# A quarter of the normalized tokens is made again from the raw tokens instead of being stored and loaded

## The chip, the core and the metric

The kernel runs on one core of one Trainium2 chip. The metric is the device time in microseconds of one execution. The core has five engines with queues of their own: TensorE (PE in the profile, with its weight loads as PEld), VectorE (DVE), ScalarE (ACT), GpSimd (POOL) and SyncE (SP), which here only issues transfers. Transfers of all queues run on 16 DMA engines.

## The reference

One step of one layer: 4096 new tokens and 64 sample tokens (8 sequences of 8), 1024 wide, all in float32.

```python
def _rmsnorm(x, g):
    xf = x.astype(jnp.float32)
    r = lax.rsqrt(jnp.mean(xf * xf, axis=-1, keepdims=True) + RMS_EPS)
    return (xf * r).astype(x.dtype) * g
...
    h = _rmsnorm(x, g_pre)
    z = h @ w_in
    cb, cc, ch, cg, q, k, v, ag, mq, mg = _split_cols(z)
    u = cc * ch
    up = jnp.concatenate([conv_buf, u], axis=1)
    conv = conv_w[0] * up[:, 0:t] + conv_w[1] * up[:, 1:t + 1] + conv_w[2] * up[:, 2:t + 2]
    out_a = jax.nn.silu(cg) * cb * conv
...
    out_b = jax.nn.silu(ag) * o_b
    o_c = _mem_attend(mq.reshape(n, t, MEM_HEADS, HEAD_DIM), mem_k, mem_v)
    out_c = jax.nn.silu(mg) * o_c
    y = jnp.concatenate([out_a, out_b, out_c], axis=-1) @ w_out
    return x + _rmsnorm(y, g_post), new_conv, new_k, new_v
```

`o_b` is windowed attention (128 keys back, with a sink for each head), `_mem_attend` is attention to 256 memory tokens. The change concerns the first two lines of the layer: the normalized tokens `h` and their product with `w_in` (1024 by 2816 columns).

## The kernel before, in words

The product `h @ w_in` is computed in three phases, each for some of the columns of `w_in`: phase 0 and phase 1 take four pairs of 128 columns each, phase 2 three (`PHASES`). In a phase, all 4160 tokens pass in 8 blocks of 520. A block's tokens, transposed so that the 1024 channels lie on the partitions, are cut into four quarters `B11`, `B12`, `B21`, `B22`: the first number says which half of the channels, the second which half of the 520 tokens. A quarter is a tile of 128 partitions by 4 by 260 elements (520 KB).

The block's product is made by Strassen's scheme in Winograd's form, with 7 products in place of 8 (`PRODUCTS`, numbered p = 0 to 6): the right operands are `B11`, `B21`, `T2`, `T3`, `T1`, `B22`, `T4`, where `T1 = B12 - B11`, `T2 = B22 - T1`, `T3 = B22 - B12` and `T4 = B21 - T2` (`t_sum`, one VectorE subtraction each). `B12` is thus no operand of a product itself: only `T1` and `T3` read it. In the first two blocks of phase 0 (`PLAIN_BLOCKS`) the eight plain products are made instead. Each operand is split into a high and a low part (`split`: a ScalarE cast to `hi`, a VectorE subtraction to `lo`), so each step p is 4 column pairs times 12 matmuls (line 368), 48 matmuls in phases 0 and 1. Two sets of `hi` and `lo` exist: the split for step p + 1 is made while step p is multiplied. The accumulated banks are taken out and added by `evict` (VectorE line 375, ScalarE line 377).

In phase 0 a quarter is loaded raw from the input (`x_load`, line 238; the input lies in chunks of 384 tokens, so a quarter comes in one or two pieces), multiplied by the gains of the norm (`gain`, line 326, four ScalarE instructions), then by the row factors `rb` (`scale`, line 335, one VectorE instruction), and stored normalized to `hd` in DRAM (POOL's queue, line 164). The row factors are made in phase 0 from sums of squares, stored to `rowd`, and spread over the partitions by a transfer (`rows_load`, line 251). For block 2 they are made in another way, by a matmul (`rows_product`), and not stored. In phase 1 the blocks 2 to 7 load their four normalized quarters from `hd` (line 530); blocks 0 and 1 make theirs as in phase 0. The differences `T1` to `T4` of phase 1 are stored to `hd` too, for phase 2.

`B12` and `B22` lie in a tile `place` with room for one block. `T3` is written over `B12` in it, so the next block's `B12` is loaded after the split of `T3`, as a job of step 4 (`next_block`). Its use is `T1`, at the end of step 6.

What sets the order: in phase 0 every engine runs in the order in which the code is written. From phase 1 on (`store_queue[0] = DMA`), stores go by SP's queue, and a scheduler with costs of its own arranges the instructions; those in `in_turn` and `keep_in_program_order` keep the place in which they were written. Each engine and queue then works strictly in that order. Small tiles of phase 1 (weight sums, convolution tiles, the row factors of block 1) come from a pool of 9 buffers (`temp`).

## Time and profile before

| | |
|---|---|
| median of 3 runs | 1526.55 us (1522.49 to 1528.41) |
| the profiled execution's own time | 1528.73 us |
| its span, first to last instruction | 1527.0 us |
| phase 0, Strassen blocks 2 to 7 | about 103 to 346 us |
| phase 1 | about 346 to 668 us, blocks 2 to 7 from about 426 us |
| phase 2 | about 668 to 936 us |
| attention and output | about 936 us to the end |
| busy: PE, PEld, DVE, ACT, POOL | 99%, 91%, 79%, 55%, 26% of the span |
| DMA | 319.71 MB, mean 209 GB/s |

The phases' times are those at which the first matmul of their operands stands in the timeline. A busy PE is not PE at its peak, since matmuls overlap; what a reader should look at is whether a matmul waits, and for whom. In the trace the names of operands are shortened: `lo_5T` is the low part of one of the differences of block 5, `x_6B` a quarter of block 6, `hd_B` a stored quarter. Names of phase 0 and phase 1 look alike, and the time tells them apart.

### The profile page before, as it was taken

What the parts mean: (1) busy time and instruction counts of PE and PEld (TensorE: products, weight loads), DVE (VectorE), ACT (ScalarE), POOL (GpSimd) and SP (SyncE); (2) the same over time, 40 slices, a digit from 0 to 9 for tenths busy, and PEclk for the clock granted to TensorE, in tenths of its full rate; (3) what the DMA queues carried; (4) which work ended last, traced back from release to release, by engine and by line L of the source; (5) the groups of instructions that cost most, each with busy time, mean ns of one, the idle gap of its engine ahead of it and who ended that gap; (6) DMA issues with size and microseconds to landing.
All of it is one profiled execution on the core that took longest, in us unless ns stands there. A gap on an engine that the chain in (4) does not pass through costs nothing.

```text
span 1527.0 us, 30947 instructions
## 1 busy us (share of the span) xinstructions
PE 1507.6 (99%) x11497; PEld 1384.4 (91%) x11497; DVE 1199.3 (79%) x2089; ACT 843.5 (55%) x2066; POOL 398.5 (26%) x576
## 2 busy tenths in 40 slices
PE   9999999999999999999999999999999999999997
PEld 8999999999999999999999999777888788888875
DVE  5779887899988777897677768777877788878874
ACT  5776665566322222354455536666666666666652
POOL 0223322211400000000111311234445544455641
PEclk9999999999999999999999999999999999999999
DMA  9989999978855333478687698988765555666552
GB/s 258 168 250 221 289 290 259 265 243 303 209 183 182 118 121 126 161 235 295 222 261 232 213 305 254 282 241 235 201 169 160 156 164 161 175 171 170 153 196 75
DMA packets 217322, 319.71 MB, mean 209 GB/s; under 512 B 37397, under 2 KB 143381, under 8 KB 217141
## 3 DMA queue, kind: packets, MB, share of 16 engines
q1 hardware_dynamic: 196837, 273.54, 60.8%
q0 software_dynamic: 19616, 43.15, 10.5%
q8 instruction: 91, 1.49, 0.4%
q10 hardware_dynamic: 720, 1.05, 0.2%
q14 instruction: 58, 0.48, 0.1%
HBM read 208.50 MB, written 110.15 MB: 209 GB/s over the span
## 4 chain that ended last, share of the span: by engine, by line
PE 75%; DMA 11%; DVE 6%; issue 4%; POOL 2%; ACT 1%; SPq 1%; DVEq 0%; ACTq 0%; POOLq 0%
PE c L368 39%; PE y_c L1746 16%; PE y L1637 3%; PE ws L1331 3%; DMA nat<-in_x_p 2%; DMA md<-th 2%; PE wo L1394 2%; PE wo L1059 2%; PE xs L1353 2%; PE xt L1366 2%; PE wt L1376 2%; PE wo L1388 2%; DMA place<-in_xt 1%; DMA wr_3A<-in_w_in 1%; DMA hd_B<-place 1%
## 5 line engine op out<-in xcount | busy, mean ns | idle before, releaser
L375 DVE TENSOR_TENSOR z<-c,z 128x520 f32<-128x520 f32 (+1 forms) x308 | 194.6, 645 | 83.5 <-PE c L368 82.5
L1746 PE MATMUL y_c<-wo,pw 128*128 128x512 f32 (+1 forms) x636 | 158.9, 392 | 0.6 <-DVE yn L1784 0.6
L1287 ACT ACTIVATE sm<-sm,wnm 128x128 f32<-128x128 f32 x256 | 99.4, 389 | 72.0 <-DVE wnm L1281 72.0
L1746 PEld LDWEIGHTS y_c<-wo,pw 128*128 128x128 f32 x636 | 114.0, 188 | 27.8 <-issue 5.4
L1190 POOL TENSOR_SCALAR xp<-xp,xrd 128x256 f32<-128x256 f32 x128 | 71.8, 577 | 196.9 <-DVE xrd L1184 192.3
L1178 ACT ACTIVATE xp<-xs,xnm 128x256 f32<-128x256 f32 x128 | 59.0, 473 | 38.3 <-DVE xnm L1170 22.9
L737 POOL CAST wmask<-negs 128x256 uint8<-128x256 f32 x1 | 1.1, 1149 | 266.6 <-DMA negs<-in_wmask 266.6
L1637 PE MATMUL y<-wo,mh 128*128 128x512 f32 x192 | 64.5, 398 | 0.2 <-ACT y L1646 0.2
L1310 POOL TENSOR_SCALAR_AFFINE_SELECT wpv<-wpt 128x512 f32<-128x512 f32 x62 | 56.9, 939 | 8.7 <-ACT wpt L1305 8.4
L1313 POOL TENSOR_SCALAR_AFFINE_SELECT wpt<-wpt 128x512 f32<-128x512 f32 x64 | 46.3, 742 | 38.6 <-ACT wpt L1305 38.2
L1331 PE MATMUL ws<-kst,q 128*128 128x256 f32 (+1 forms) x480 | 55.7, 297 | 0.0
L1341 DVE COPY_PREDICATED sm<-wmask,ws 128x512 f32<-128x512 uint8 x60 | 40.5, 729 | 19.0 <-ACT sm L1340 19.0
L276 ACT ACTIVATE nat<-nat 104x1024 f32<-104x1024 f32 x40 | 42.3, 1058 | 23.6 <-DMA nat<-in_x_p 23.5
L1658 DVE SCALAR_TENSOR_TENSOR xr<-yn,yst,xr 128x1024 f32<-128x1024 f32 (+2 forms) x35 | 51.3, 1470 | 2.9 <-POOL yst L1653 2.8
L407 ACT CAST zh<-z 128x520 fp32r<-128x520 f32 x56 | 33.3, 624 | 34.6 <-DVE z L375 31.9
L377 ACT COPY z<-c 128x520 f32<-128x520 f32 (+1 forms) x44 | 24.4, 554 | 50.5 <-PE c L368 47.2
L1331 PEld LDWEIGHTS ws<-kst,q 128*128 128x128 f32 (+1 forms) x480 | 46.4, 187 | 4.1
L1287 ACT ACTIVATION_READ_ACCUMULATOR sm<-sm,wnm 128x1 f32 x256 | 47.9, 187 | 0.0
L1295 DVE TENSOR_TENSOR sm<-sm,wrd 128x512 f32<-128x512 f32 x64 | 44.5, 696 | 1.1
L1746 PE MATMUL y_c<-wo,pc 128*128 128x512 f32 (+1 forms) x162 | 45.2, 400 | 0.0
L164 POOL DMA_DIRECT2D md<-th x48 | 26.3, 549 | 71.3 <-DVE th L425 61.0
L1637 PEld LDWEIGHTS y<-wo,mh 128*128 128x128 f32 x192 | 36.1, 188 | 8.9 <-issue 1.0
(1037 smaller groups left out, 5556.9 us busy)
## 6 DMA issues: line engine op xcount, KB each, us to landing
q<-qd SPq DMA_DIRECT2D x168, 128.0 KB
xr<-in_x_p SPq DMA_DIRECT2D x32, 512.0 KB
nat<-in_x_p SPq DMA_DIRECT2D x39, 416.0 KB
o_yp<-xr SPq DMA_DIRECT2D x31, 512.0 KB
kst<-qd SPq DMA_DIRECT2D x112, 128.0 KB
md<-th POOLq DMA_DIRECT2D x48, 260.0 KB, 7.2
qd<-zh SPq DMA_DIRECT2D x48, 260.0 KB
qd<-z SPq DMA_DIRECT2D x48, 260.0 KB
```

The costliest lines, as they stand in the source:

```text
L368: TE.matmul(bank[:, :HW], l, r, start=first and i == 0, stop=last and i == 3 * KH - 1)
L375: add = lambda dst, other: V.tensor_tensor(dst, c, other, op=ALU.add)
L1178: S.activation(p[:, i, :], s[:, i, :], AF.Exp, bias=nm[:, i : i + 1], scale=SCALE, accum_out=den[:, i : i + 1])
L1190: G.tensor_scalar(p[:, i, :], p[:, i, :], self.rds[h][:, i : i + 1], 0.5, op0=ALU.mult, op1=ALU.mult)
L1287: S.activation(sm[:, hh, :], sm[:, hh, :], AF.Exp, bias=nm[:, hh : hh + 1], scale=SCALE, accum_out=den[:, hh : hh + 1])
L1295: V.tensor_tensor(sm, sm, rd.unsqueeze(2).to_broadcast([P, 4, P]), op=ALU.mult)
L1310: G.affine_select(pv.rearrange("p (h q) -> p h q", h=4), p3, pattern=[[0, 4], [-1, P]], compare_op=ALU.is_gt, fill=0.0, base=0, channel_mu ...
L1313: G.affine_select(p3, p3, pattern=[[0, 4], [1, P]], compare_op=ALU.is_ge, fill=0.0, base=0, channel_multiplier=-1)
L1331: TE.matmul(out(kvh, col, bank), q(kvh, col, bank)[r], k(kvh, part)[r], start=first, stop=True, skip_group_check=not first, **place)
L1637: TE.matmul(acc, self.hl[l][:, k], wo[k][p][:, r], start=k + i == 0, stop=k + i == KT + 1)
L1658: x = V.scalar_tensor_tensor(self.xr[:m, cs], yn[:m, cs], st[:m, 3:4], self.xr[:m, cs], op0=ALU.mult, op1=ALU.add)
L1746: TE.matmul(acc, a[:, l, k], w[:, r, cs], start=first, stop=k == len(ws) - 1 and i == 2, skip_group_check=not new)
```

## The change

`hd` has no `B12` any more. In phase 0 the blocks 2 to 7 don't store it (six transfers of 520 KB fewer on POOL's queue), and block 2 now stores its row factors as well. In phase 1 the blocks 2 to 7 load `B12` raw, spread the row factors (one transfer of 260 KB for each block, at step 1), and multiply by gains and factors at step 6, like blocks 0 and 1.

```diff
@@ -71,7 +71,7 @@
-    hd = [{o: tc.dram_tile([P, KH, HW], F32, name=f"hd{b}_{o}") for o in ("B12", *(o for _, o in PRODUCTS))}
+    hd = [{o: tc.dram_tile([P, KH, HW], F32, name=f"hd{b}_{o}") for _, o in PRODUCTS}
           for b in range(NBLK)]
@@ -283,10 +283,8 @@
             if b in (0, PLAIN_BLOCKS):
                 nat["factors"] = r
-            if b == PLAIN_BLOCKS:
-                return
             G.dma_start(rowd[b].rearrange("(i p) -> p i", p=RG), r[:RG, 0:5])
-            if b > 0:
+            if b > 0 and b != PLAIN_BLOCKS:
                 row_spreads[b] = 4
@@ -333,7 +331,7 @@
     def scale(x, b, o):
         rb = rows[b][:, HW * (int(o[2]) - 1) : HW * int(o[2])]
         in_turn(V.tensor_tensor(x, x, rb.unsqueeze(1).to_broadcast([P, KH, HW]), op=ALU.mult))
-        if b >= PLAIN_BLOCKS or o != "B12":
+        if o != "B12":
             store(hd[b][o], x)
@@ -522,8 +520,12 @@
+    def is_raw(ph, b, o):
+
+        return ph == 0 or b < PLAIN_BLOCKS or o == "B12"
+
     def x_of(ph, b, o, parts=KH):
-        if ph == 0 or b < PLAIN_BLOCKS:
+        if is_raw(ph, b, o):
             t = x_load(ph, b, o, parts)
         else:
             t = x_tile(ph, b, o)
@@ -531,11 +533,11 @@
     def x_gain(ph, b, o):
-        if ph == 0 or b < PLAIN_BLOCKS:
+        if is_raw(ph, b, o):
             gain(xs[ph, b][o], o)
     def x_scale(ph, b, o):
-        if ph == 0 or b < PLAIN_BLOCKS:
+        if is_raw(ph, b, o):
             scale(xs[ph, b][o], b, o)
@@ -556,7 +558,7 @@
-        if p == 1 and nph == 1 and nb < PLAIN_BLOCKS:
+        if p == 1 and nph == 1:
             jobs.append(lambda: rows_load(nb, nb > 0))
```

Up to the new function `is_raw` the changed kernel's lines have numbers 2 lower, behind it 2 higher: gain, scale, split and evict are lines 324, 333, 356 and 357, and 373. In the rows below, a name like `x1_5B21` is phase 1, block 5, quarter B21, and the last number only tells tiles apart; `z1_4_0_1` is an output tile of block 4, `c1_4_0_6` the bank of its step 6, `ub`, `tail`, `cacc` belong to the convolution, `ws10` to the weight sums for phase 2.

SP's queue in phase 1, block 1 (steps 2 to 4), where the weight sums are loaded. Before:

```order
L166 DMA md_149<-cacc0_0_5169 128x456
L201 DMA ws10A21_5335<-in_w_in 128x512
L201 DMA ws10A22_5337<-in_w_in 128x512
L201 DMA ws10A11_5339<-in_w_in 128x512
L201 DMA ws10A12_5341<-in_w_in 128x512
L530 DMA place_159<-hd2_B12_99 128x1040
L166 DMA hd1_T4_98<-x1_1B21_4884 128x1040
L166 DMA md_149<-cacc0_1_5264 128x456
L530 DMA x1_2B21_5374<-hd2_B21_101 128x1040
```

and now:

```order
L166 DMA md_141<-cacc0_0_5156 128x456
L251 DMA rb2_5262<-rowd2_77 128x520
L201 DMA ws10A21_5324<-in_w_in 128x512
L201 DMA ws10A22_5326<-in_w_in 128x512
L201 DMA ws10A11_5328<-in_w_in 128x512
L201 DMA ws10A12_5330<-in_w_in 128x512
L238 DMA place_151<-in_xt 128x4x172
L166 DMA hd1_T4_96<-x1_1B21_4871 128x1040
L166 DMA md_141<-cacc0_1_5224 128x456
L532 DMA x1_2B21_5363<-hd2_B21_98 128x1040
L238 DMA place_151<-in_xt 128x4x88
```

The spread of the row factors stands ahead of the loads of the weight sums, and the second piece of `B12` stands behind the load of `B21`. In the blocks after it the spread stands at the same step, and the one or two pieces of `B12` stand where the one load stood.

ScalarE in phase 1, at the end of block 4 (step 6), for block 5. Before:

```order
L438 ACTIVATE cth4_0_6922<-z1_4_0_0_6618 128x520
L358 CAST hi1_5B11_6905<-x1_5B11_6608 128x4x260
L438 ACTIVATE cth4_1_6938<-z1_4_2_0_6645 128x520
L471 ACTIVATE cacc4_0_7009<-ub4_0_7004,convw_71 128x520
L358 CAST hi1_5B21_6970<-x1_5B21_6787 128x4x260
```

and now:

```order
L436 ACTIVATE cth4_0_6935<-z1_4_0_0_6628 128x520
L356 CAST hi1_5B11_6918<-x1_5B11_6618 128x4x260
L436 ACTIVATE cth4_1_6951<-z1_4_2_0_6655 128x520
L324 ACTIVATE place_151<-place_151,gpre_61 128x260 x4
L356 CAST hi1_5B21_6988<-x1_5B21_6799 128x4x260
L469 ACTIVATE cacc4_0_7027<-ub4_0_7022,convw_71 128x520
```

The four gains stand ahead of the cast of `B21`, and the convolution's first product has moved behind that cast.

VectorE at the same place. Before:

```order
L375 TENSOR_TENSOR z1_4_0_1_6530<-c1_4_0_6_6909,z1_4_0_1_6530 128x2x260
L446 SCALAR_TENSOR_TENSOR z1_4_0_0_6618<-z1_4_0_1_6530,z1_4_0_0_6618 128x520
L456 TENSOR_TENSOR ub4_0_7004<-z1_4_0_0_6618,z1_4_0_1_6530 128x520
L458 COPY tail4_0_7007<-ub4_0_7004 128x2
L455 COPY ub4_1_7029<-tail3_1_6588 128x2
L473 SCALAR_TENSOR_TENSOR cacc4_0_7009<-ub4_0_7004,convw_71,cacc4_0_7009 128x520
L375 TENSOR_TENSOR z1_4_2_1_6570<-c1_4_2_6_6941,z1_4_2_1_6570 128x2x260
L348 TENSOR_TENSOR x1_5T1_6967<-place_159,x1_5B11_6608 128x1040
L359 TENSOR_TENSOR lo1_5B21_6971<-x1_5B21_6787,hi1_5B21_6970 128x4x260
L348 TENSOR_TENSOR x1_5T2_6988<-place_159,x1_5T1_6967 128x1040
```

and now:

```order
L373 TENSOR_TENSOR z1_4_0_1_6540<-c1_4_0_6_6922,z1_4_0_1_6540 128x2x260
L333 TENSOR_TENSOR place_151<-place_151,rb5_6682 128x1040
L444 SCALAR_TENSOR_TENSOR z1_4_0_0_6628<-z1_4_0_1_6540,z1_4_0_0_6628 128x520
L454 TENSOR_TENSOR ub4_0_7022<-z1_4_0_0_6628,z1_4_0_1_6540 128x520
L373 TENSOR_TENSOR z1_4_2_1_6580<-c1_4_2_6_6954,z1_4_2_1_6580 128x2x260
L346 TENSOR_TENSOR x1_5T1_6985<-place_151,x1_5B11_6618 128x1040
L357 TENSOR_TENSOR lo1_5B21_6989<-x1_5B21_6799,hi1_5B21_6988 128x4x260
L346 TENSOR_TENSOR x1_5T2_7006<-place_151,x1_5T1_6985 128x1040
L456 COPY tail4_0_7025<-ub4_0_7022 128x2
L471 SCALAR_TENSOR_TENSOR cacc4_0_7027<-ub4_0_7022,convw_71,cacc4_0_7027 128x520
```

The scaling of `B12` has come in ahead of the convolution's gate, and two copies and the convolution's second product have moved from ahead of `T1` to behind `T2`. The matmuls stand in the same order as before.

## The prediction

> **What bounds the kernel.** I read the busy times by stretch first. In the fence the columns are the stretch, its length, the busy us of PE, PEld, DVE, ACT and POOL with the number of instructions, PE's clock, the share of the DMA engines and GB/s. The first row is phase 0 and the start of phase 1, the next three are block 1 of phase 1, and the last holds most of the blocks whose `B12` changes.
>
> ```profile
> 110.00:395.00 285.00, 282.79 (x2373) 281.75 (x2373) 249.03 (x308) 174.76 (x303) 77.61 (x121) 1.00 0.92 256
> 395.00:400.00 5.00, 5.00 (x44) 5.00 (x44) 5.00 (x9) 1.07 (x1) 4.66 (x7) 1.00 1.12 89
> 400.00:420.00 20.00, 19.71 (x166) 19.50 (x165) 16.79 (x26) 4.51 (x5) 4.67 (x5) 1.00 0.93 326
> 420.00:425.00 5.00, 5.00 (x44) 5.00 (x43) 4.20 (x7) 1.60 (x2) 0.00 (x0) 1.00 0.02 7
> 440.00:640.00 200.00, 200.00 (x1669) 200.00 (x1668) 155.13 (x212) 55.13 (x65) 0.00 (x0) 1.00 0.41 140
> ```
>
> PE is busy in 200.00 of 200 us of phase 1 and in 282.79 of 285 us of phase 0. In phase 0 the DMA engines are 92% busy; in phase 1 they are 41% busy, VectorE 78% (155.13 of 200), ScalarE 28%. So TensorE bounds both phases, and what the change can win or lose is what TensorE waits for. I read its waits next: first from 100 to 400 us (in all: us, times, longest), then from 395 to 700 us, where there is one.
>
> ```profile
> PE c L368 <- DVE lo_6B L359: 0.9, 1, 0.9
> PE c L368 <- ACT hi_6B L358: 0.9, 1, 0.9
> PE c L368 <- DVE lo_2T L359: 0.3, 1, 0.3
> PE c L368 <- DVE lo_5T L359: 0.2, 1, 0.2
> ```
>
> ```profile
> PE c L368 <- DVE lo_1B L359: 0.3, 1, 0.3
> ```
>
> Phase 0 has 0.9 + 0.9 + 0.3 + 0.2 = 2.3 us to win, phase 1 and the start of phase 2 have 0.3 us. Third, the chain of work that ended last, which joins a run of matmuls into one row (start, length, instructions):
>
> ```profile
> 114.99 20.10 PE c L368 x167
> ...
> 401.63 8.75 DMA ws10A<-in_w_in
> 413.56 1.25 DVE lo_1B L359
> ```
>
> ```profile
> 414.85 296.79 PE c L368 x2471
> ```
>
> From 414.85 us on TensorE never lets go for 296.79 us. But its pace differs: 296.79 us / 2471 = 120.1 ns a matmul there, 20.10 / 167 = 120.4 ns in the earlier row, where the last matmul's length (0.28 us, rows below) is spread over few; without it 120.0 and 118.7 ns. The granted clock is 1.00 in both stretches. So the same matmul runs at two paces, and the slower one sets in right behind the short wait for `lo_1B`. I come back to that among the rivals.
>
> **Removed: six stores of 520 KB in phase 0.** The stores go by POOL's queue, the loads that TensorE's two longest waits hang on by SP's. From 240 to 300 us the queues' shares of the 16 engines were (q1 is SP's, q0 POOL's), and the third row counts the stores from `place`, with KB of one and us to landing; six of the 13 go:
>
> ```profile
> q1 hardware_dynamic: 7956, 8.28, 49.9%
> q0 software_dynamic: 2213, 7.49, 42.4%
> ```
>
> ```profile
> hd_B<-place POOLq DMA_DIRECT2D x13, 520.0 KB, 10.0
> ```
>
> Before the waits of block 6 the raw loads of `place` were issued by SP and landed late at ScalarE's gains (start, length, engine, the idle time before it and what ended it):
>
> ```profile
> 245.66 1.98 SPq L238 DMA_DIRECT2D place<-in_xt  x2
> ...
> 252.12 1.87 SPq L238 DMA_DIRECT2D place<-in_xt  x2
> ```
>
> ```profile
> 259.92 1.73 ACT L326 ACTIVATE place<-place,gpre 128x260 f32<-128x260 f32 x4 [1.86 <-DMA place<-in_xt]
> ...
> 265.78 1.72 ACT L326 ACTIVATE place<-place,gpre 128x260 f32<-128x260 f32 x4 [0.20 <-DMA place<-in_xt]
> ```
>
> The first load took 259.92 - 245.66 = 14.3 us, and ScalarE's wait made the cast of `x_6B` behind it late. One store less is 532,480 B / 256 GB/s = 2.1 us less in a queue that is full, more than the 1.86 us that ScalarE waited. In POOL's order the store of block 5's `B12` lies ahead of these loads. So I let both waits of 0.9 us go: -1.8 us. The ends: 0, if the time is lost in SP's queue and not in the engines, and -2.3 us, if all four waits go. I take nearly the second, since both queues' shares add up to 92% of the same engines. The Trainium skill (DMA: Bandwidth & Descriptors, Rules for kernel authors) says that spreading transfers over the queues of SP, ACT and GpSimd brings no bandwidth, since all run on the same 16 engines. By that rule the -1.8 us stands; were the queues apart, this term would be 0 and the sum 1.8 us higher. The trace agrees as far as two shares that add up to 92.3% can show it. In block 2 the store of five row factors to `rowd` comes in on POOL, which is 27% busy there (77.61 of 285); nobody in phase 1 needs it for 300 us: 0.
>
> **Added on ScalarE and VectorE: gains and scaling in phase 1.** Phase 0 shows the same instructions on the same tile (ns: least, median, most):
>
> ```profile
> L326 ACT ACTIVATE place<-place,gpre x64: 495/498/516, 95.3 to 385.3; 128x260 f32<-128x260 f32 x64
> ...
> L335 DVE TENSOR_TENSOR place<-place,rb x16: 1231/1234/1244, 97.0 to 386.9; 128x1040 f32<-128x1040 f32 x16
> ```
>
> Six blocks take 6 x (4 x 0.498) = 12.0 us on ScalarE and 6 x 1.234 = 7.4 us on VectorE. Whether they delay a split is read from block 5, where VectorE worked nearly without a pause:
>
> ```profile
> 544.66 0.69 DVE L375 TENSOR_TENSOR z<-c,z 128x520 f32<-128x520 f32 x1
> ...
> 548.18 0.69 DVE L375 TENSOR_TENSOR z<-c,z 128x520 f32<-128x520 f32 x1
> 548.79 1.23 DVE L348 TENSOR_TENSOR x_5T<-place,x_5B 128x1040 f32<-128x1040 f32 x1
> 549.93 1.24 DVE L359 TENSOR_TENSOR lo_5B<-x_5B,hi_5B 128x1040 fp32r<-128x1040 f32 x1
> 551.09 1.23 DVE L348 TENSOR_TENSOR x_5T<-place,x_5T 128x1040 f32<-128x1040 f32 x1
> ...
> 554.94 1.24 DVE L359 TENSOR_TENSOR lo_5T<-x_5T,hi_5T 128x1040 fp32r<-128x1040 f32 x1
> ```
>
> ```profile
> 542.76 0.63 ACT L438 ACTIVATE cth<-z 128x520 f32<-128x520 f32 x1
> ```
>
> ```profile
> 553.19 0.28 PE L368 MATMUL c<-lo_5B,w_0A 128*128 128x260 f32 x1
> ```
>
> ```profile
> 558.95 0.28 PE L368 MATMUL c<-lo_5T,w_0S 128*128 128x260 f32 x1
> ```
>
> The low part of `B21` is ready at 549.93 + 1.24 = 551.17 and first read at 553.19: 2.0 us to spare. The low part of `T2` is ready at 556.18 and read at 558.95: 2.8 us. Starts follow each other by 1.15 us for a whole quarter and 0.61 for an output tile. In the new order, from the eviction at 544.66: scaling starts at 545.3, the gate at 546.4, `ub` 547.0, the eviction 547.6, `T1` 548.3, the low part of `B21` 549.4, `T2` 550.6 (the next at 551.7). Because two copies and the convolution's product moved behind `T2`, the low part of `B21` and `T2` are 0.5 us earlier than before. Behind `T2` these and five others (0.1 + 0.7 + 0.6 + 0.7 + 0.1 + 0.6 + 0.6 + 0.1) take 3.5 us: the low part of `T2` starts at 555.2, 0.3 us later, with 2.5 us left. The scaling waits for the gains, 542.76 + 0.63 + 4 x 0.5 = 545.4, just when VectorE gets there. So the cover is the 2.0 us ahead of step 1, and the term is 0. Its ends are 0 and, if gains come d later than 545.4, 6 x (d - 2.0) us.
>
> Is `B12` in the tile by then? SP issued its load long before:
>
> ```profile
> 408.57 0.33 SPq L530 DMA_DIRECT2D place<-hd_B  x1
> ...
> 441.43 0.33 SPq L530 DMA_DIRECT2D place<-hd_B  x1
> ```
>
> ```profile
> 421.81 0.63 ACT L438 ACTIVATE cth<-z 128x520 f32<-128x520 f32 x1
> ```
>
> For block 2 the gains follow at 421.81 + 0.63 = 422.4, and the DMA engines, 2% busy from 420 us, had nothing left by then. For block 3 a load as slow as the 14.3 us in phase 0, from 441.43, would land at 455.7, and one step of block is 48 x 0.12 = 5.8 us, so a block later the gains begin at 422.4 + 7 x 5.8 = 463: 7 us to spare. The raw load has runs of 1040 B and less where `hd` had 4160 B; short pieces are 12, 36, 88 and 112 tokens (48, 144, 352 and 448 B). The Trainium skill (DMA: Bandwidth & Descriptors, Specifications) asks for 512 B or more for line rate, below which a read-modify-write is done. By that rule, as an estimate, those four pieces, counted as 512 B a run, cost 512 x 1056 B more, 0.5 MB in four blocks or about 0.4 us each at 326 GB/s, which the 7 us hold; by the row of block 2 too, so the sum is the same by either. No run here yet shows such a load in phase 1.
>
> **Added: the spread of the row factors, 260 KB a block.** In blocks 3 to 7 it lies in DMA engines that are 41% busy, at no cost. In block 1 it stands ahead of the weight sums' loads, and there TensorE's 0.3 us begins:
>
> ```profile
> 410.40 0.69 DVE L204 TENSOR_TENSOR ws10S<-ws10A,ws10A 128x512 f32<-128x512 f32 x1 [2.46 <-DMA ws10A<-in_w_in]
> ...
> 413.56 1.24 DVE L359 TENSOR_TENSOR lo_1B<-place,hi_1B 128x1040 fp32r<-128x1040 f32 x1
> ```
>
> ```profile
> 414.85 0.39 PE L368 MATMUL c<-lo_1B,w_0S 128*128 128x260 f32 x1 [0.29 <-DVE lo_1B L359]
> ```
>
> VectorE waits 2.46 us for the weights, five instructions later `lo_1B` is late, and TensorE waits. 266,240 B more in front of them are 0.8 us at the 326 GB/s of 400 to 420 us, and 3.0 us at the 89 GB/s of the stretch ahead. The loads run in the former, so +0.8 us; ends 0 (if the spread gets through beside others) and +3.0 us.
>
> **Sum.** Against the profiled execution, 1528.73 us: -1.8 + 0 + 0.8 = -1.0, so 1527.7 us. The median of the runs, 1526.55 us, is 2.2 us below it; from there the forecast is 1525.5 us. No change, that is.
>
> **Rivals.**
> *The pace of the matmuls turns.* 2471 matmuls at 120.0 rather than 118.7 ns are 3.2 us, and a short wait came just ahead of the turn. If phase 1 keeps 118.7 ns, the time is 1525.5 - 3.2 = 1522.3 us; if phase 0 takes 120.0 ns from about 115 us on (300 us, 2500 matmuls), 1528.8 us. For it: the turn at 414 us. Against it: phase 0 had four waits, and its average, (285.00 - 2.3) / 2373 = 119.1 ns with a few records missing, is still under phase 1's 200.00 / 1669 = 119.8 ns. Chance 0.2 and 0.1.
> *The gains hold up VectorE.* The scaling is pinned between two evictions. If `B12` lands so late that gains come 4 us behind 545.4, each of six blocks loses 4 - 2 = 2 us: 1525.5 + 12 = 1537.5 us, slower. It decides at 2.0 us late for the first loss, and at 2.0 + (1534.2 - 1525.5) / 6 = 3.5 us for half a percent. For it: strict order on both engines. Against it: 7 us to spare. Chance 0.10.
> *More is won than the waits show.* All 2.3 us of phase 0, phase 1 at the fast pace, and no wait for `lo_1B`: 1526.55 - 2.3 - 3.2 - 0.3 = 1520.8; half a percent takes 1.9 us more, from runs that scatter by 5.9 us (1522.49 to 1528.41). Chance 0.06.
>
> That the change does not do what it says is excluded: the orders show the stores gone and the raw loads in their place.
>
> **How the numbers follow.** The forecast has 0.54, with 1523 to 1529.5 us as its own range (ends of its terms: 1526.55 - 2.3 and 1526.55 + 3.0, and scatter). The range over the cases leaves out the outer parts of the two last rivals: 1518.5 to 1535 us. Half a percent is 7.6 us, about what a measurement of this kernel can tell from no change: under 1518.9 us is faster, over 1534.2 us slower. The pace alone does not reach either. So faster 0.06, slower 0.10, same 0.84.
>
> **What would show it.** In the changed profile: TensorE busy in all of 440 to 640 us, and no wait for `lo_6B` and `hi_6B` near 264 us (removal right); a wait for `lo_1B` of about 1.1 us near 415 us (spread right; 0.3 or none: wrong); gains in phase 1 that wait for no load, and scalings that wait less than 2 us for gains; DMA in phase 0 below 92%. The prediction is wrong if TensorE's waits repeat in each block of phase 1, or if time moves in phase 2 or the attention, where no instruction is added.

## The result, and the profile after

| | before | after |
|---|---|---|
| median on one chip, 22 runs each | 1523.41 us (1519.89 to 1529.59) | 1527.74 us (1524.01 to 1534.48) |
| ratio after / before | | 1.0027, 95% interval 1.0015 to 1.0038 |
| the profiled execution | 1528.73 us | 1525.57 us |

The change makes the kernel 0.27% slower, about 4 us, where the forecast was 1.0 us faster. That is inside the half percent that was called "no change" and inside the forecast's range, but the interval leaves out 1, and the sign is not the one forecast. That 1527.74 us lies in the range is in part luck: the forecast started from the median of three runs, 1526.55 us, and that was 3.1 us above the median of 22; 1.0 us less than the latter would have been 1522.4 us. The profiled execution is one of the faster ones of the changed kernel, and that of before one of the slower ones of its kernel. So the two traces can't be compared by their ends: what follows compares them place by place, and leaves the totals to the medians.

The busy times by stretch, of after (same columns as in the prediction):

```profile
110.00:395.00 285.00, 283.77 (x2384) 283.29 (x2383) 251.62 (x310) 175.22 (x305) 73.55 (x117) 1.00 0.90 249
400.00:420.00 20.00, 19.24 (x161) 19.03 (x160) 16.86 (x24) 4.10 (x5) 3.99 (x5) 1.00 0.97 341
440.00:640.00 200.00, 200.00 (x1688) 200.00 (x1687) 160.95 (x220) 63.94 (x88) 0.00 (x0) 1.00 0.44 150
```

TensorE still bounds both phases. Phase 1 has 200.00 of 200 us as before, VectorE has 5.8 us more work there and ScalarE 8.8 us, and neither shows in TensorE. Its waits, of after, from 100 to 400 us and then from 395 to 700 us:

```profile
PE c L366 <- ACT hi_2B L356: 1.9, 1, 1.9
PE c L366 <- DVE lo_2B L357: 1.6, 2, 0.9
PE c L366 <- DVE lo_2T L357: 0.5, 1, 0.5
```

```profile
PE c L366 <- DVE lo_1B L357: 0.8, 1, 0.8
```

The two waits of 0.9 us for block 6 are gone and the one for `lo_1B` has grown, as forecast. But there is a new place: TensorE waits 1.9 + 1.6 = 3.5 us for the first operands of block 2, where before had no wait. Nothing that the prediction priced lies there. ScalarE's rows show who is late. The first row is of before, the second of after: the square of a piece of the tokens (`nat`), which ScalarE does for the row factors.

```profile
93.72 1.06 ACT L276 ACTIVATE nat<-nat 104x1024 f32<-104x1024 f32 x1 [1.38 <-DMA nat<-in_x_p]
```

```profile
97.28 1.06 ACT L276 ACTIVATE nat<-nat 104x1024 f32<-104x1024 f32 x1 [7.18 <-DMA nat<-in_x_p]
```

ScalarE waits 7.18 us for a load of raw tokens instead of 1.38. Behind that square, in ScalarE's written order, stand the gains and the casts of block 2 that TensorE needs at 103 us. The load doesn't belong to the change. What the change put ahead of it is the store of block 2's row factors, here in POOL's row of after:

```profile
80.35 0.99 POOL L286 DMA_DIRECT2D rowd<-r  x1 [0.30 <-POOL r L283]
```

And this is what the DMA engines did from 84 to 104 us, in slices of half a microsecond: the share of time in which they were busy in tenths, and the GB/s they moved. First before, then after:

```profile
DMA  9655479999999978797730099459999999997787
GB/s 312 205 165 203 181 227 281 333 326 318 336 339 251 217 133 262 238 303 238 180 115 0 0 90 149 66 156 287 354 283 399 383 424 374 333 316 307 313 288 255
```

```profile
DMA  9999991078968965899584999788788978761092
GB/s 274 298 273 280 312 175 51 25 29 41 108 109 55 63 48 29 41 52 122 147 185 157 403 296 263 221 222 273 299 316 324 324 281 304 230 181 49 33 131 90
```

From 87 to 93.5 us those of after move 25 to 122 GB/s where those of before moved 133 to 339. Except in the first microsecond they are 50 to 90% busy all the same. The queues' rows of these 6.5 us (packets, MB, share of the 16 engines) show with what; first before, then after:

```profile
q1 hardware_dynamic: 2264, 1.78, 97.9%
```

```profile
q1 hardware_dynamic: 602, 0.39, 71.5%
```

In after it is SP's loads alone; the queue of the store, POOL's, has no packet there. But one packet of the loads takes 0.715 x 16 x 6.5 us / 602 = 124 ns, where before it took 0.979 x 16 x 6.5 us / 2264 = 45 ns, for somewhat fewer bytes. So it is not the store's own packets that fill the engines: the loads' packets behind it have become slow. The store is 2 KB, in 520 pieces of 4 B: the factors lie across 104 partitions and five columns, and in memory each stands beside one of another partition. It landed 13.6 us after its issue, at about 94 us, which is when the stretch ends:

```profile
rowd<-r POOLq DMA_DIRECT2D x1, 2.0 KB, 13.6
```

### The profile page after: what moved, and what is told of

Read it like the earlier page. It is cut to its first block, busy times and chain, and to the rows that moved or that the text cites. A ratio compares the mean times of both kernels' runs of the same rounds, so it can differ in the third digit from the quotient of the medians.

```text
span 1523.9 us, 30992 instructions
## 1 busy us (share of the span) xinstructions
PE 1504.7 (99%) x11497; PEld 1382.7 (91%) x11497; DVE 1203.5 (79%) x2095; ACT 850.6 (56%) x2090; POOL 392.0 (26%) x571
## 4 chain that ended last, share of the span: by engine, by line
PE 76%; issue 6%; DVE 4%; DMA 4%; POOL 2%; ACT 1%; SPq 1%; DVEq 0%; POOLq 0%; ACTq 0%
PE c L366 40%; PE y_c L1748 17%; PE ws L1333 3%; PE y L1639 3%; PE wo L1396 2%; PE wo L1061 2%; PE xs L1355 2%; PE xt L1368 2%; PE wt L1378 2%; PE wo L1390 1%; PE mem_acc L792 1%; DMA ws10A<-in_w_in 1%; POOL md L164 1%; DMA vd<-v 1%; PE y L1634 0%
```

## The experiments

The first theory (A) was that the 520 pieces of 4 B hold up the loads behind them at a place without cover. Its rivals: the new work in phase 1 costs the time (B), or the missing stores shift everything else (C). Each run below stands against runs of the kernel before on the same chip, between 1521.3 and 1523.4 us in the median.

**One part alone, or one part undone.** First, the kernel before with nothing but block 2's store of factors, which nobody reads there:

```diff
-            if b == PLAIN_BLOCKS:
-                return
             G.dma_start(rowd[b].rearrange("(i p) -> p i", p=RG), r[:RG, 0:5])
-            if b > 0:
+            if b > 0 and b != PLAIN_BLOCKS:
```

> The kernel before with one transfer more: block 2's row factors are stored to DRAM (520 elements of 4 bytes), nothing reads them. Theory A (this store of tiny pieces blocks the full DMA queues near 80 us, a token load behind it lands late, ScalarE's gains and casts for block 2 wait behind it in strict order, and TensorE waits some 3.5 us near 103 to 114 us more than before): slower by 2.5 to 4.5 us. Theory B (the work added in phase 1 costs the time) and theory C (the removed stores shift phase 0's transfers and turn the matmuls to their slower pace): within 1 us of the kernel before.

Measured: 1.0023 (1.0010 to 1.0036), 1527.42 us. This one transfer of 2 KB costs 3.5 us (0.0023 x 1523.4), nearly the whole loss. Its waits of TensorE for block 2, and ScalarE's row:

```profile
PE c L366 <- ACT hi_2B L356: 3.0, 1, 3.0
PE c L366 <- DVE lo_2B L357: 0.9, 1, 0.9
```

```profile
99.78 1.06 ACT L276 ACTIVATE nat<-nat 104x1024 f32<-104x1024 f32 x1 [8.06 <-DMA nat<-in_x_p]
```

Second, the kernel before without its six stores of `B12`, and with another quarter loaded in its place in phase 1:

```diff
-        if b >= PLAIN_BLOCKS or o != "B12":
+        if o != "B12":
             store(hd[b][o], x)
...
-            DMA.dma_start(t, hd[b][o])
+            DMA.dma_start(t, hd[b]["B11" if o == "B12" else o])
```

> The kernel before without the six stores of B12 of blocks 2 to 7; phase 1 loads those blocks' B11 in the place of B12, so all its differences with B12 are computed from the wrong quarter, at the same cost. Theory A: faster by 1 to 2.5 us, since TensorE's two waits near 264 us go, as forecast. Theory B: the same. Theory C: slower by 2 to 4 us, with matmuls 1.3 ns apart more in phase 0 or 1.

Measured: 0.9982 (0.9971 to 0.9992), a gain of 2.7 us (1.2 to 4.4). Rival C falls: taking the stores away loses nothing by itself, it wins in the mean. The fastest runs are alike, though, 1519.53 us here and 1519.06 us in before: what e2 lacks is the slower runs of before. Whether the stores make those, or the pace of the matmuls that is told of below, was not separated. The loss is of another kind: the fastest run of e1 (1523.84 us) is 4.8 us above that of before on its chip, and that of the changed kernel (1524.01 us) 4.1 us.

Third, the changed kernel with `B12` stored all the same:

```diff
-        if o != "B12":
+        if b >= PLAIN_BLOCKS or o != "B12":
             store(hd[b][o], x)
```

> The changed kernel, but B12 is still stored in phase 0 and the store is never read. Theory A: slower than the kernel before by 3 to 6 us (the tiny store, the later weight sums in phase 1, and no relief at 264 us). Theory B: slower by 4 to 6 us, with the loss in phase 1. Theory C: the same as the kernel before, or the 0.8 us of the row factors' spread.

Measured: 1.0026 (1.0009 to 1.0044). It is as slow as the changed kernel. By e2 it should have been about 2.7 us slower than that; the two intervals, of 1.7 us and more to each side, are too wide to say whether the stores' cost is still there. Its profiled execution, the fastest of its 12 runs, shows the cover: ScalarE waits 3.39 us for the tokens and TensorE only 0.2 us for block 2.

Fourth, the changed kernel with block 2 as before (its `B12` stored and loaded, its factors not stored), and the blocks 3 to 7 changed:

```diff
-        if o != "B12":
+        if b == PLAIN_BLOCKS or o != "B12":
             store(hd[b][o], x)
...
-        return ph == 0 or b < PLAIN_BLOCKS or o == "B12"
+        return ph == 0 or b < PLAIN_BLOCKS or o == "B12" and b > PLAIN_BLOCKS
...
-        if p == 1 and nph == 1:
+        if p == 1 and nph == 1 and nb != PLAIN_BLOCKS:
```

> The changed kernel, but block 2 is treated as before: its B12 is stored and loaded, its row factors are neither stored nor spread; blocks 3 to 7 are made again from the raw tokens. Theory A: the loss goes, and the kernel is 0 to 2 us faster than the one before. Theory B: five sixths of the loss stay, 3 to 4 us slower. Theory C: 2 to 4 us slower.

Measured: 0.9987 (0.9976 to 0.9998), 1521.39 us. This version beats both kernels in the mean, the one before by 2.0 us (0.3 to 3.7; as with e2, the fastest runs are no faster) and, against a ratio from another chip, the changed one by some 6 us. Five of the six stores are gone, five blocks make `B12` in phase 1, and it is faster: rival B falls. From 100 to 700 us TensorE has one wait left, the old one behind block 2's differences:

```profile
PE c L368 <- DVE lo_2T L359: 0.3, 1, 0.3
```

**The same factors in another form.** If it is the pieces, the whole change must do without the loss when the store is written otherwise. In the next kernel block 2's factors are stored from the tile in which they lie spread over all partitions, one row of it, just behind the copy that makes it:

```diff
+            if b == PLAIN_BLOCKS:
+                return
             G.dma_start(rowd[b].rearrange("(i p) -> p i", p=RG), r[:RG, 0:5])
...
         S.copy(rows[b].rearrange("p (a n) -> p a n", a=2), acc)
+        if b == PLAIN_BLOCKS:
+            G.dma_start(rowd[b].rearrange("(a n) -> a n", a=1), rows[b][0:1, :])
```

> The changed kernel, whole, but block 2's row factors are stored from the tile in which they lie spread already: one partition's row, 13 pieces of 160 bytes, in place of 520 pieces of 4 bytes, at the same place of the queue. Theory A (the tiny pieces block the transfers behind them): the loss goes, and this is 1 to 2.5 us faster than the kernel before. Theory B2 (the loss lies in what else block 2 got, the spread ahead of the weight sums and the raw load): 3 to 5 us slower than before, like the change.

Measured: 0.9997 (0.9985 to 1.0009). The loss is gone; against the changed kernel's 1.0027, which was measured on another chip, this is 0.30%, 4.6 us. ScalarE's wait for the tokens is 2.45 us and TensorE has none for `hi_2B` or `lo_2B`.

The kernel of e1 with the same 520 factors in 104 pieces of 20 B, one for each partition:

```diff
-            G.dma_start(rowd[b].rearrange("(i p) -> p i", p=RG), r[:RG, 0:5])
+            G.dma_start(rowd[b].rearrange("(p i) -> p i", i=5) if b == PLAIN_BLOCKS else rowd[b].rearrange("(i p) -> p i", p=RG), r[:RG, 0:5])
```

> The kernel before with the unread store of block 2's row factors as 104 pieces of 20 bytes. Theory A by number of pieces (104 for 520): 0 to 1 us slower than the kernel before. Theory A2 (any store on that queue at that place delays what is behind it, whatever its pieces): 3 to 5 us slower, as with 4-byte pieces.

Measured: 0.9994 (0.9978 to 1.0009). No loss. The DMA engines of this kernel, from 84 to 104 us, show no stretch of low GB/s under load; at 93 us they are empty for a microsecond, as in before at 94.5 us:

```profile
DMA  9979999989887866410019698999899955785265
GB/s 185 201 194 324 334 329 320 287 259 225 147 184 188 287 238 246 147 49 0 0 58 240 174 248 322 430 405 415 349 391 282 215 149 215 305 330 239 91 74 131
```

**Twice, and elsewhere.** The kernel of e1 with the store issued twice, into a buffer of its own as well:

```diff
             G.dma_start(rowd[b].rearrange("(i p) -> p i", p=RG), r[:RG, 0:5])
+            if b == PLAIN_BLOCKS:
+                G.dma_start(row_again.rearrange("(i p) -> p i", p=RG), r[:RG, 0:5])
```

> The kernel before with the unread store of 520 pieces of 4 bytes twice, to two places. Theory A by number of pieces: 7 to 12 us slower than the kernel before, since the cover is used up by the first store. Theory A2 (the queue, not the pieces): 4 to 5 us slower.

Measured: 1.0052 (1.0032 to 1.0071), 7.9 us. Twice the pieces, about twice the loss. ScalarE, then TensorE, then the DMA engines from 84 to 104 us:

```profile
103.06 1.06 ACT L277 ACTIVATE nat<-nat 104x1024 f32<-104x1024 f32 x1 [11.62 <-DMA nat<-in_x_p]
```

```profile
PE c L369 <- ACT hi_2B L359: 6.5, 1, 6.5
PE c L369 <- DVE lo_2B L360: 0.7, 1, 0.7
```

```profile
DMA  9999999990337555949679999999499946589786
GB/s 200 243 277 315 290 263 200 83 52 0 20 31 14 19 36 53 66 50 29 10 29 47 91 124 88 26 37 63 83 121 129 112 135 206 182 312 312 246 231 258
```

Low throughput (0 to 135 GB/s) now lasts from 87.5 to 100.5 us, 13 us where after had 6.5.

The kernel before with the same 520 pieces of 4 B stored in phase 1, from a copy of five numbers of each of 104 partitions of a token tile:

```diff
+    def quiet_store():
+        q = tiny.tile([P, 8], F32, tag="quiet", name="quiet", bufs=1)
+        G.tensor_scalar(q[:RG, 0:5], xs[1, 5]["B11"][:RG, 0, 0:5], 1.0, 0.0, op0=ALU.mult, op1=ALU.add)
+        G.dma_start(rowd[PLAIN_BLOCKS].rearrange("(i p) -> p i", p=RG), q[:RG, 0:5])
...
+        if (ph, b, p) == (1, 4, 5):
+            jobs.append(quiet_store)
```

> The kernel before with a store of 520 pieces of 4 bytes to the same place in DRAM, but in phase 1 near 525 us, where the transfers have pauses (GpSimd copies five numbers a partition of a token tile of block 5 and stores them; nothing reads them). Theory A: within 0.7 us of the kernel before, since nothing that TensorE needs stands behind it. If a store of tiny pieces costs TensorE its time anywhere: 3 to 5 us slower.

Measured: 0.9999 (0.9987 to 1.0010). The store starts at 511.7 us, and the engines show the same thing from 508 to 528 us, with other loads behind it in the queues:

```profile
DMA  9879999960300079971035299710099879999982
GB/s 333 133 283 424 399 433 399 370 237 8 4 1 0 0 316 408 158 17 8 0 17 33 25 216 137 250 25 21 0 166 141 216 208 366 383 416 416 424 366 92
```

Here the loads come a step of a block ahead of their use, and TensorE waits for none. So the store holds up transfers wherever it is, and costs time only where a load behind it is nearly late already.

**The term of the spread, and the other stores.** The kernel of e5 with the spread of the factors in phase 1 issued two steps later, behind the loads of the weight sums:

```diff
-        if p == 1 and nph == 1:
+        if p == (1 if nb < PLAIN_BLOCKS else 3) and nph == 1:
```

> As e5 (the changed kernel with block 2's factors stored from the spread tile in 13 pieces of 160 B), and the phase-1 spread of a block's factors is issued at step 3 instead of step 1, so that in block 1 it lies behind the weight loads. If the spread ahead of ws10A costs (predicted 0.8 us, TensorE's wait for lo_1B went from 0.3 to 0.8 us), that wait is back at 0.3 us or less and the ratio to before falls from e5's 0.9997 towards e4's 0.9987: 0.9985 to 0.9992. If the spread costs nothing, 0.9997 again and the same wait for lo_1B as in e5.

Measured: 0.9995 (0.9980 to 1.0011), with a wait of 0.4 us for `lo_1B`. e5's profiled execution had none at that place. The run tells nothing apart: a term of half a microsecond is below what these runs resolve, and the wait itself comes and goes.

The kernel before with all its stores of factors in pieces of 20 B:

```diff
-            G.dma_start(rowd[b].rearrange("(i p) -> p i", p=RG), r[:RG, 0:5])
+            G.dma_start(rowd[b].rearrange("(p i) -> p i", i=5), r[:RG, 0:5])
```

> The kernel before, with every store of row factors (blocks 0, 1 and 3 to 7) written as 104 pieces of 20 B instead of 520 pieces of 4 B; the factors stand in another order in rowd, so the output is not the reference's, the work is the same. If any 4 B store in phase 0 costs TensorE time as block 2's did (4 us where the cover is thin), up to 0.9 us near 264 us and 0.3 us at other places may go: ratio 0.998 to 0.9995. If only the place near 80 us has no cover, the stores that were there before are hidden: 1.000 within 0.001.

Measured: 0.9995 (0.9981 to 1.0008). The seven stores of 520 pieces of 4 B that were there before cost nothing that can be seen. But each of them slows the loads just as block 2's does. These are the GB/s from 140 to 160 us, around one of the seven, of before and then of e11:

```profile
GB/s 365 232 272 255 330 332 266 145 283 242 175 17 42 33 42 25 8 25 50 108 58 76 150 150 138 171 253 177 371 352 371 437 363 409 425 391 361 379 377 386
```

```profile
GB/s 435 312 225 283 366 204 391 241 191 100 25 0 158 399 366 147 197 348 328 184 111 391 233 374 391 250 383 333 141 116 197 324 234 169 162 175 259 316 394 430
```

From 145.5 us on, before moves 8 to 108 GB/s for 5.5 us; e11 is as low for 1.5 us. Such a stretch follows all seven stores in before and none in e11: in the six microseconds behind a store (from 1 us after the middle one of its packets) the engines move 60 to 96 GB/s in before and 173 to 255 GB/s in e11. From 110 to 395 us they are 92% busy in before and 83% in e11, both at 256 GB/s. So the seven stand where the cover holds, and this is why the profile of before gave no wait from which the price could have been read.

**How many pieces, how small, how near.** By now "number of pieces" explained every run. Two more kernels were to show it, both of them the kernel before with another store in block 2's place: one column only, 104 pieces of 4 B, and 520 pieces of 20 B of a constant.

```diff
             if b == PLAIN_BLOCKS:
+                G.dma_start(rowd[b][:RG].rearrange("(i p) -> p i", p=RG), r[:RG, 0:1])
                 return
```

> The kernel before, with a store in block 2 of one column of factors only: 104 pieces of 4 B. e1 (520 pieces of 4 B) lost 0.23% (3.5 us), e6 (104 pieces of 20 B) nothing. If the number of pieces decides, this one loses nothing: 1.000 within 0.0015, and TensorE has no wait for hi_2B near 103 us. If it is that pieces of 4 B are worse than pieces of 20 B, a fifth to all of the loss stays: 1.0005 to 1.0025.

```diff
+    row_wide = tc.dram_tile([10 * HW], F32, name="row_wide")
...
             if b == PLAIN_BLOCKS:
+                G.dma_start(row_wide.rearrange("(i p c) -> p i c", p=RG, c=5), ident[:RG, 0:25].rearrange("p (i c) -> p i c", c=5))
                 return
```

> The kernel before, with a store in the same place of 520 pieces of 20 B (10.4 KB of a constant into a buffer that nobody reads). If the number of pieces decides, it loses as e1 did: 1.0015 to 1.0035, with ScalarE's wait for nat near 92 us at 7 us or more and TensorE's for hi_2B at 2 us or more. If pieces of 4 B are what hurts, 1.000 within 0.0015.

Measured: e12 1.0028 (1.0016 to 1.0040), e13 0.9995 (0.9982 to 1.0008). This is the opposite of what the number of pieces asks for: 104 pieces of 4 B lose 4.3 us, and 520 pieces of 20 B, ten kilobytes, nothing. ScalarE's row and the GB/s from 84 to 104 us, of e12 and then of e13:

```profile
98.42 1.06 ACT L276 ACTIVATE nat<-nat 104x1024 f32<-104x1024 f32 x1 [6.52 <-DMA nat<-in_x_p]
```

```profile
GB/s 259 194 211 169 228 297 330 313 313 303 201 70 84 87 65 60 18 1 36 102 95 78 25 99 134 255 386 230 271 222 273 300 374 341 333 347 271 254 131 98
```

```profile
94.13 1.06 ACT L277 ACTIVATE nat<-nat 104x1024 f32<-104x1024 f32 x1 [2.86 <-DMA nat<-in_x_p]
```

```profile
GB/s 224 155 196 293 267 281 224 259 264 266 110 168 274 205 206 205 229 205 164 41 25 199 383 399 258 240 108 273 306 322 338 181 132 66 205 353 246 207 283 300
```

What is left is the 4 B themselves, or that 4 B pieces of neighbouring partitions lie side by side in memory. So e12 again, once with its pieces 512 B apart, once with two columns, which makes them 8 B:

```diff
+    row_far = tc.dram_tile([104 * 128], F32, name="row_far")
...
+                G.dma_start(row_far.rearrange("(p c) -> p c", c=128)[:, 0:1], r[:RG, 0:1])
```

> As e12 (the kernel before with a store of 104 pieces of 4 B in block 2), but the pieces lie 512 B apart in memory. If the size of the pieces decides, it loses as e12 did: 1.0015 to 1.004, with ScalarE's wait for nat near 92 us at 6 us or more and TensorE's wait for hi_2B over 1 us. If it is many engines writing small pieces into the same few lines of memory, nothing is lost: 1.000 within 0.0015.

```diff
+    row_two = tc.dram_tile([104 * 2], F32, name="row_two")
...
+                G.dma_start(row_two.rearrange("(p c) -> p c", c=2), r[:RG, 0:2])
```

> As e12, but with two columns of factors in 104 pieces of 8 B side by side. If the loss goes down smoothly with the size of a piece, or with the number of pieces that share a line, about half of e12's is left: 1.0005 to 1.002. If 4 B is a case by itself: 1.000 within 0.0015; the two can be told apart only by the traces (GB/s from 88 to 96 us, ScalarE's wait for nat).

Measured: e14 1.0008 (0.9992 to 1.0024), e15 0.9991 (0.9974 to 1.0008). The same two rows, of e14 and then of e15:

```profile
95.12 1.06 ACT L277 ACTIVATE nat<-nat 104x1024 f32<-104x1024 f32 x1 [2.85 <-DMA nat<-in_x_p]
```

```profile
GB/s 235 271 337 256 199 218 306 321 311 305 330 335 278 223 152 209 199 172 229 229 164 66 25 150 416 408 266 223 215 223 347 338 297 124 124 91 172 369 280 240
```

```profile
93.19 1.06 ACT L277 ACTIVATE nat<-nat 104x1024 f32<-104x1024 f32 x1 [2.17 <-DMA nat<-in_x_p]
```

```profile
GB/s 240 248 250 307 301 301 303 174 105 80 76 132 90 246 270 188 246 180 213 123 57 349 391 275 239 165 247 246 347 348 357 183 214 345 238 207 308 299 190 90
```

Apart from each other the 4 B pieces leave the throughput alone in the profiled execution, and the wait is 2.85 us. At 8 B the throughput falls to 76 to 132 GB/s for 2.5 us, where 4 B took 6.5, and the cover holds. This points to small pieces written side by side, and not to small pieces as such. The interval of e14's ratio overlaps that of e12's, but the traces hold more than these stores, since every kernel except e11 keeps the seven old ones. Over all 16 profiled executions, in the six microseconds counted as above, the engines moved 33 to 127 GB/s behind the 112 stores of 4 B side by side, e12's among them, and 168 to 258 GB/s behind the 13 others: pieces of 160 B (e5, e9), 20 B (e6, e11, e13), 8 B (e15), and 4 B apart (e14). The two do not overlap. So that it is the form of the store is shown, and that 20 B are harmless; for 4 B apart there is the one store of e14. Why 4 B side by side are bad stays open: e7 against e1 and e12 (twice the loss for twice the pieces, the same loss for a fifth of them) doesn't fit a simple count.

**The cover, measured.** Over all profiled executions, ScalarE's wait for the tokens in that row and TensorE's waits for `hi_2B` and `lo_2B` together go like this (us):

| kernel | ScalarE waits for `nat` | TensorE waits for block 2's quarters |
|---|---|---|
| before, e2, e4, e5, e6, e8, e11, e14, e15 | 0 to 2.9 | 0 |
| e13 | 2.9 | 0.9 |
| e9, e3 | 3.2, 3.4 | 0.3, 0.2 |
| e12 | 6.5 | 2.3 |
| after | 7.2 | 3.5 |
| e1 | 8.1 | 3.9 |
| e7 | 11.6 | 7.2 |

In the four last rows the difference is 4.2, 3.7, 4.2 and 4.4 us. About 4 us of a late load is covered in these, and from there on TensorE pays microsecond for microsecond. Of the 4 us of cover before had used 1.4. The 4 us are not the same in every execution: e13 lost 0.9 us where e14, as late, lost nothing.

**Behind a long wait.** The waits are not the whole price. In e7 TensorE waited 6.5 us, up to 108.83 us; at 106.0 us its granted clock fell to 0.50 and stayed there for 10.2 us. These are two stretches of 4 us of e7 (columns as in the prediction):

```profile
112.00:116.00 4.00, 4.00 (x20) 4.00 (x20) 4.00 (x5) 2.51 (x5) 3.08 (x4) 0.50 0.92 276
120.00:124.00 4.00, 4.00 (x36) 4.00 (x35) 4.00 (x5) 4.00 (x7) 1.07 (x2) 1.00 1.06 133
```

At half the clock TensorE did 20 matmuls in the time of 36. In e1 and e12 the clock was at 0.50 for 3.4 us, from 106.5 and 105.7 us on, next to their waits for block 2; in the profiled execution of after it was not. Over all runs the mean granted clock is 0.9971 in the changed kernel (22 runs), 0.9949 in e7, and 0.9978 to 0.9980 in the five sets of before. As an estimate from these, (0.9979 - 0.9971) x 1523 us = 1.2 us of the change's loss of 4 us went this way. That the wait brings the lower clock on is what the order in time suggests; no run here shows it by itself.

## Why the prediction was wrong

**The step that failed** is in the part on the removed stores: "In block 2 the store of five row factors to `rowd` comes in on POOL, which is 27% busy there [...]; nobody in phase 1 needs it for 300 us: 0." It asked who waits for POOL and who waits for the factors, and both answers were right: nobody. It didn't ask what stands behind the store in the 16 engines that all queues share, though the same paragraph had just read them as 92% full. Behind it stood a load of tokens for which ScalarE waited already in before (1.38 us), and behind that ScalarE's strict order up to the operands of block 2. The term is +3.5 us by e1 alone and +4.6 us by the changed kernel against e5 (on two chips), not 0. Counted in bytes the store really is nothing (2 KB, 0.01 us at 256 GB/s): that it slows the loads for 6 us could not be worked out from its size. But the trace of before showed it seven times, in stretches of few GB/s at busy engines as the one from 145.5 us under e11. And this is how long the seven stores of that kind took to land in it:

```profile
DMA to landing us min/median/max: 9.3/11.3/15.6
```

That is 11.3 us in the median for 2 KB, where the stores of 520 KB took 10.0; in e11, in pieces of 20 B, it is 3.7 us. No rival had this mechanism; the two that ended slower lay elsewhere.

The Trainium skill (DMA: Bandwidth & Descriptors, Specifications) gives 512 B as the least size for line rate, below which a read-modify-write is done. The prediction weighed that rule for the pieces of the raw load and not for this store. The traces agree on the direction only: pieces of 20 B are far below 512 B as well, and 520 of them cost nothing (0.9995), while 104 of 4 B cost 0.28%. The Trainium skill (DMA: Bandwidth & Descriptors, Why small descriptors are slow) counts a fixed overhead for each packet and for each operation. By that alone e13, with five times the pieces, would be dearer than e12, and the runs show the reverse.

**The removal: right in sign; its size came from one execution.** The waits of block 6 are gone, and ScalarE's gains wait for no load any more there (two rows of ScalarE of after, at the place of the waits of 1.86 and 0.20 us):

```profile
256.98 1.71 ACT L324 ACTIVATE place<-place,gpre 128x260 f32<-128x260 f32 x4
...
262.12 1.71 ACT L324 ACTIVATE place<-place,gpre 128x260 f32<-128x260 f32 x4
```

e2 puts the six stores at 2.7 us (1.2 to 4.4), which holds the 1.8. But the size can't be read from the two waits: none of the ten other kernels that keep all six stores (e1, e3, e6, e7, e8, e11 to e15) shows a wait for block 6 in its profiled execution. The wait was one of that execution of before, and that 1.8 fits e2's average is in part luck. The full queue on which the term was built was not full of bytes alone either: with the seven stores of factors in 20 B the same stretch is 83% busy at the same 256 GB/s (e11).

**Gains and scaling in phase 1: right, 0.** The order that was forecast, counted from the eviction ahead of the scaling, came out to a tenth of a microsecond. VectorE of after, block 5:

```profile
543.96 0.69 DVE L373 TENSOR_TENSOR z<-c,z 128x520 f32<-128x520 f32 x1
544.57 1.23 DVE L333 TENSOR_TENSOR place<-place,rb 128x1040 f32<-128x1040 f32 x1
...
548.70 1.23 DVE L357 TENSOR_TENSOR lo_5B<-x_5B,hi_5B 128x1040 fp32r<-128x1040 f32 x1
549.85 1.23 DVE L346 TENSOR_TENSOR x_5T<-place,x_5T 128x1040 f32<-128x1040 f32 x1
...
554.39 1.23 DVE L357 TENSOR_TENSOR lo_5T<-x_5T,hi_5T 128x1040 fp32r<-128x1040 f32 x1
```

The low part of `B21` starts 548.70 - 543.96 = 4.74 us behind the eviction (forecast 549.4 - 544.66 = 4.74), `T2` 5.89 (5.94), the low part of `T2` 10.43 (10.54). No wait of TensorE in phase 1's blocks 2 to 7; the rival of late gains did not happen, and e4 and e5 leave no room for it.

**The spread: +0.8 us is neither shown nor refuted.** VectorE's wait for the weights and the low part of `B12` of block 1, of after:

```profile
411.12 0.69 DVE L204 TENSOR_TENSOR ws10S<-ws10A,ws10A 128x512 f32<-128x512 f32 x1 [2.79 <-DMA ws10A<-in_w_in]
...
414.27 1.23 DVE L357 TENSOR_TENSOR lo_1B<-place,hi_1B 128x1040 fp32r<-128x1040 f32 x1
```

The wait for the weights went from 2.46 to 2.79 us, TensorE's from 0.3 to 0.8: +0.5 us, not +0.8. This is within what one execution differs from the next: e3 and e5, with the spread in the same place as after, show no such wait.

**The sum.** Without the failed step the change is e5: -0.5 us (-2.3 to +1.4) where the sum said -1.0. With it, 1.0027.

**The pace of the matmuls** did turn in the profiled execution, as the first rival had it. The chain of after has the same 2471 matmuls as before in one piece behind the wait for `lo_1B`:

```profile
415.56 293.65 PE c L366 x2471
```

293.65 / 2471 = 118.8 ns, where before had 120.1. In after this run of matmuls begins 0.7 us later than in before and ends 2.4 us earlier, at 709.2 us. That is most of why the profiled execution of the slower kernel ends 3.2 us earlier. But the change is not needed for it: in the profiled executions phase 1, from 460 us on, ran at 120 ns in before, e1, e7 and e13, and near 118.5 in e2, e6, e8, e11, e12, e14 and e15, and all of these have the phase 1 of before (in e2 with another quarter loaded, in e8 with one store more). All five with the new phase 1 (after, e3, e4, e5, e9) had the faster pace; whether the change favours it, five executions can't say. In after the slow pace had held from 351 us up to the wait for `lo_1B`, where in before it set in.

## What to carry to other kernels

A transfer is priced by what it does to the transfers behind it in the shared engines, not by its bytes nor by who waits for its result: first look for a load that is nearly late behind the place where it goes in, and at how much cover is left there. In the trace of the kernel as it is, look for stretches in which the engines are busy and few bytes move, and for what was issued ahead of them. A small store from many partitions should not put one element of each beside the next; turned so that each partition writes 20 B in one piece (or a spread copy is stored from one partition), the same 520 numbers cost nothing that could be measured. And where a change brings one part that costs and another that wins, build it without the smallest part too: here the version with one block left as it was is, in the mean, faster than both.

## What the runs showed of the hardware

A store of 104 pieces of 4 B side by side, 416 B in all, kept the 16 DMA engines at 1 to 102 GB/s for 6.5 us (e12), although loads of hundreds of KB were on their way. 520 such pieces do the same for 6.5 us (after), two stores of 520 for 13 us (e7), and 104 of 8 B brought it down to 76 to 132 GB/s for 2.5 us (e15). It is the packets of the loads behind the store that become slow: 124 ns for one in place of 45 ns (after against before, 87 to 93.5 us). Over the 16 profiled executions the engines moved 33 to 127 GB/s in the six microseconds behind the 112 such stores of 4 B, and 168 to 258 GB/s behind the 13 stores of another form.

The granted clock of TensorE fell from 1.00 to 0.50 during its wait of 6.5 us in e7, for 10.2 us, and for 3.4 us next to the shorter waits of e1 and e12. At 0.50 it did 20 matmuls in 4 us, at 1.00 36.

The same matmul with 260 columns follows the one before it by 118.7 or by 120.0 ns at the same granted clock of 1.00, for hundreds of microseconds, and changes between the two at some of TensorE's short waits. Near 415 us it turned to the slower pace in before and to the faster one in after. Over the 2471 matmuls behind that place this is 3.2 us, nearly as much as the whole change. What sets the pace was not tried. The Trainium skill (TensorE: Matmul & The Clock Gate, Back-to-back issue gap) gives N / 2.4 + 2.5 ns as the gap of an isolated matmul, by estimate 110.8 ns for 260 columns, and for a stream of weight loads and matmuls about 81 ns at 128 columns and 131 ns at 512. Both paces lie between these two, and the section names no second pace for one size.
